# Attention scores with full-depth products per component

## The chip, the cores and the metric

The kernel runs on one core of one Trainium2 chip. The metric is the device time of one execution in microseconds, the median of several runs. The core has five engines with queues of their own: TensorE (PE, matmuls; its weight loads are listed apart as PEld), VectorE (DVE), ScalarE (ACT), GpSimd (POOL) and SyncE (SP), which issues most DMA transfers. Each engine takes its instructions in a fixed order.

## The reference, cut to what matters

The reference is a decoder layer on 1024 rows of 1024 channels: three branches for token mixing (differential attention, retention, a gated linear recurrence) merged by gates, then cross-attention, then an MLP. The change touches the scores of the differential attention. It has eight heads; each has two components of 64 channels for queries and keys and one value of 128 channels. For each block of 128 queries:

```python
s = jnp.einsum('bqhcd,bkhcd->bhcqk', q_blk, k).astype(jnp.float32) * scale
s = jnp.where(causal, s, -jnp.inf)
p = jax.nn.softmax(s, axis=-1)
a = p[:, :, 0] - lam * p[:, :, 1]
return jnp.einsum('bhqk,bkhe->bqhe', a.astype(v.dtype), v)
```

All of it is in float32. The kernel feeds TensorE with float32 numbers in two rounded parts (a "Split": hi and lo, whose sum is the number) and adds several products: for a plain product hi x hi, hi x lo and lo x hi.

## The kernel before, in words

`run` goes through the stages in order: retention, then `attention`, then the recurrence and the gates (`h_products`), the branch products, cross-attention and the MLP. Here only `attention` matters, from about 304 to 766 us of the trace.

`attention` goes over eight heads (h) and, in each, over eight query blocks of 128 rows (i). `diff_scores(h, i)` makes the two score matrices of a block, one for each component, of n = 128 (i + 1) columns, in accumulators of two PSUM banks each (tag "sc", two in all), adds the causal mask to the last 128 columns (L462), finds the row maximum (L464), takes the exponential into an SBUF tile of 4 KB per partition (tag "p", L467; the row sums come along), scales (L469, L472) and joins both components (L473). The joined matrix stays in the first component's tile until it is transposed. `diff_trans(h, j)` (L487) transposes the matrices of blocks 2j and 2j + 1 once both are there, in the step of block 2j + 2, for the last pair in the step of the next head's first block. `diff_av` multiplies with the values, `diff_out` normalises the result, with a few small transfers through DRAM.

The queries and keys of a head come from `diff_qk`: a projection of 24 products on 512 columns for each half of the rows, into PSUM tiles "psk". The keys are kept in tiles of 128 partitions (tag "kd"): for the first component hi in the lower 64 partitions and lo in the upper ones, for the second one the other way round (L430, L431). The queries (tag "qd", two tiles) hold three planes of 512 columns: hi of the first component twice, in both halves of the partitions, hi of the second likewise, and one plane with lo of both, the first component's in the lower 64 partitions, the second's in the upper ones. ACT writes hi (L441), DVE subtracts to get lo (L442), and a DMA on SP's queue copies hi to the other half of the partitions (L443).

So a score block of up to 512 columns takes four products. Two have depth 128 (L457), one for each component: hi of the queries, twice, against hi over lo of the keys. Two have depth 64 (L460): lo of the queries against hi of the keys, the first component's in partitions 0 to 63, the second's in 64 to 127.

Between the score steps the projections of the next head (`diff_qk`, `diff_v`) are put in at given blocks (`FILL`). The order in which each engine gets its instructions is not that of the code alone: a planner takes them by priority (the code's order) as its own model finds them ready, and gives out the places of the tile pools at the same time. A tile's place can be taken again when its last reader is through. `wdma`, `wsplit` and the like keep some instructions in the code's order.

Of the kernel before, what the change touches and what calls it, by code (L numbers as in the profile page):

```python
# [17 lines left out]
P = 128  # L18
# [7 lines left out]
# columns of the per-channel vector table  # L26
# [13 lines left out]
class Split:  # L40
    """An f32 operand as an exact sum of two f32r parts."""
# [8 lines left out]
class Kernel:  # L50
# [17 lines left out]
    def split(self, dst, src, lo_engine=None):  # L68
        """src f32 in SBUF or PSUM -> dst Split"""
        ins = self.nc.scalar.copy(dst.hi, src)  # L70
        self.lo_ins = (lo_engine or self.nc.vector).tensor_tensor(dst.lo, src, f32(dst.hi), op=ALU.subtract)  # L71
        return ins

    def after(self, key, ins):
        """keep the instructions of one key, all of one engine, in program order"""
        prev = self.last.get(key)
        if prev is not None:
            self.tc.add_manual_dep(
                ins.ins, prev.ins.name, mybir.DependencyInfo(mybir.DependencyClass.NoSync, mybir.DependencyReason.DATA),
                reason="program order")  # L80
        self.last[key] = ins

    def weight(self, unit, kts, pool=None, tag="w", wbufs=2, dst=None, lo=None):
        """a [128, 1024] weight unit -> Split of [128, kts, 1024 // kts]"""
        st = self.stage.tile([P, D], F32, tag="st", name="st")
        self.after("wdma", self.nc.sync.dma_start(st, unit))
        w = dst
        if dst is None:
            w = (pool or self.wpool).tile([P, 2, D], F32R, tag=tag, name=tag, bufs=None if pool is None else wbufs)
        s = Split(w[:, 0, :], w[:, 1, :])  # L90
        self.after("wsplit", self.split(s, st, lo or self.nc.gpsimd))
        return Split(*[p.rearrange("p (k c) -> p k c", k=kts) for p in (s.hi, s.lo)])

    def rstd(self, dst, src, scale, eps):
        """dst = (src * scale + eps) ** -0.5 on [128, few]"""
        self.nc.vector.tensor_scalar(dst, src, scale, eps, op0=ALU.mult, op1=ALU.add)
        self.nc.gpsimd.tensor_tensor(dst, dst, self.mhalf[:, : dst.shape[-1]], op=ALU.pow)

    def norm_rows(self, xt, gain, work, bufs=2):
        """normalise the rows of xt [128, 1024]"""  # L100
        nc = self.nc
        xs = work.tile([P, D], F32, tag="xs", name="xs", bufs=bufs)
        ss = self.small.tile([P, 1], F32, tag="ss", name="ss", bufs=4)
        nc.scalar.activation(xs, xt, AF.Square, accum_out=ss)
        rs = self.small.tile([P, 1], F32, tag="rs", name="rs", bufs=4)
        self.rstd(rs, ss, 1.0 / D, 1e-6)
        self.norm_ins = nc.vector.scalar_tensor_tensor(xs, xt, rs, gain, op0=ALU.mult, op1=ALU.mult)
        return xs

    def rows_T(self, xs, dst, psum, key=None):  # L110
        """xs [128, 1024] transposed into dst, two Splits [128, 4, 128]"""
# [9 lines left out]
    def later(self, f=None, depth=1):  # L121
        """put off f until the tensor engine has had other work; run what was put off before the last `depth`"""
        if f is not None:
            self.put_off.append(f)
        while len(self.put_off) > (depth if f is not None else max(0, len(self.put_off) - 1)):
            self.put_off.pop(0)()
            if f is None:
                break
# [39 lines left out]
    def scalars(self):  # L168
        """lambda of the differential attention, its output gains"""
# [20 lines left out]
    def softplus(self):  # L190
        """softplus of the LRU's parameter, times its factors"""
# [7 lines left out]
        # log1p(z) = 2 atanh(z / (2 + z)), 0 <= z <= 1  # L199
# [18 lines left out]
    def norm_x(self, work):  # L218
        """h^T, the normalised input; a generator, one step per 128 rows"""
# [21 lines left out]
    # retention, one chunk of one head at a time, in stages  # L241
    def ret_proj(self, h, n, c):
# [5 lines left out]
        # rotary  # L248
# [7 lines left out]
        # the keys' decay is put into the values, the queries' into the norm  # L256
# [43 lines left out]
    def ret_out(self, h, n, c):  # L300
# [3 lines left out]
        # group norm  # L304
# [28 lines left out]
    def retention(self, pool):  # L333
        """retention without its gate, led by the norm of its input"""
# [33 lines left out]
    def h_sums(self, kt, half, hp):  # L368
        """the sums of blocks of h^T that its block products need, to DRAM"""
# [26 lines left out]
    def proj_T(self, w, half, ps):  # L396
        """out^T [128 columns, 512 rows]"""
        self.mmk(ps, [(w[:, kt, :], self.hT[half][kt // 4][:, kt % 4, :]) for kt in range(KT)])

    # differential attention  # L400
    def diff_v(self, pr):
        """the projections of two heads' values, in four steps"""
# [13 lines left out]
    def diff_qk(self, h):  # L416
        """the projections of a head's queries and keys, in four steps"""
# [5 lines left out]
        for half in range(2):  # L423
            ps = self.ps.tile([P, HB], F32, tag="mm", name="psk")
            self.proj_T(w, half, ps)
            # of the first component hi over lo, of the second lo over hi
# [7 lines left out]
        for half in range(2):  # L434
            ps = self.ps.tile([P, HB], F32, tag="mm", name="psk")
            self.proj_T(w, half, ps)
            # hi of each component twice, lo of both
            t = ap.tile([P, 3, HB], F32R, tag="qd", name="qd", bufs=2)
            q.append(t)
            for c, (x, y) in enumerate(((lower, upper), (upper, lower))):  # L440
                nc.scalar.activation(t[x, c, :], ps[x, :], AF.Copy, scale=0.125)  # L441
                v.scalar_tensor_tensor(t[x, 2, :], ps[x, :], 0.125, f32(t[x, c, :]), op0=ALU.mult, op1=ALU.subtract)  # L442
                nc.sync.dma_start(f32(t[y, c, :]), f32(t[x, c, :]))  # L443
            yield

    def diff_scores(self, h, i):
# [7 lines left out]
        for b in range((n + HB - 1) // HB):  # L454
            e = min(HB, n - b * HB)
            for c, sc in enumerate(scs):
                nc.tensor.matmul(sc[:, b * HB:b * HB + e], lhsT=qt[:, c, cols], rhs=k[b][:, c, 0:e], start=True, stop=False)  # L457
            for c, sc in enumerate(scs):
                x = slice(64 * c, 64 * c + 64)
                nc.tensor.matmul(sc[:, b * HB:b * HB + e], lhsT=qt[x, 2, cols], rhs=k[b][x, c, 0:e], start=False, stop=True)  # L460
        for sc in scs:
# [3 lines left out]
            p = ap.tile([P, S], F32, tag="p", name="p", bufs=5)  # L465
# [80 lines left out]
    def attention(self):  # L546
# [18 lines left out]
        for h in range(8):  # L565
            # the rest of this head's projections, then the next one's
# [81 lines left out]
    def h_products(self):  # L648
        """the LRU's projections and scan, retention's gate, the merge gates: block products with h^T;
        a generator: the first two steps need no pools of their own"""  # L650
# [8 lines left out]
        # which sums of blocks of the branches' inputs go with which pair  # L659
# [80 lines left out]
    def o_sums(self, i, q, sp):  # L740
        """the sums of blocks of a branch's input that its block products need, to DRAM: T1, T3 and T4, T2"""
# [14 lines left out]
    def load_blocks(self, i, tile):  # L756
        """the right factors of a branch: even tiles of channels first, then odd ones; a generator, one step a block"""
# [13 lines left out]
    def fill_block(self, b, x, tile):  # L771
        """a [128, 4, 512] of DRAM, split"""
# [5 lines left out]
    def gates(self, count, pool, tag):  # L778
        """the next merge gates, to DRAM; two steps a gate"""
# [13 lines left out]
    def branch(self, order, i, right, bw, st, sps, nxt):  # L793
        """a branch's product, gated, added to those before it; then the next one's right factors, or the sum split"""
# [46 lines left out]
    def w_out(self, half, mT, w, hx, work, psum):  # L841
        """from here on to the last norm the second half of the rows comes first"""
# [22 lines left out]
    def block(self, pool):  # L865
        """a Split of [128, 4, 512]"""
# [3 lines left out]
    def mem_slot(self):  # L870
        kv, hm = (s.tile([P, 2, 2, D], F32R, tag="s", name="kvox") for s in (self.slotA, self.slotB))
        # keys, values; the normalised memory first, then the attention's output
# [29 lines left out]
    # cross-attention, one head of half the rows at a time, in stages  # L902
# [42 lines left out]
    def xa_out(self, st, cb, g):  # L945
        """half a tile of rows of the cross-attention's output, the MLP's norm"""
# [14 lines left out]
    # the MLP's right factors come from the even (B11, B21) and the odd (B12, B22) tiles of rows  # L961
# [26 lines left out]
    def mlp_t4(self, i, g):  # L988
        """T4 of a tile of rows, once there is room for it"""
# [8 lines left out]
    def xattn(self, hx, work, psum):  # L998
        """the memory's keys and values, the cross-attention; ends with rows still to transpose"""
# [7 lines left out]
        def SC(u):  # L1007
            """the scores of head u, the transposes of the one before"""
# [48 lines left out]
    # 2 x 2 block products with seven multiplications (Winograd's form);  # L1057
    # left factors: A11 A12 S4 A22 S1 S2 S3, right factors: B11 B21 B22 T4 T1 T2 T3, T4 with its sign turned
# [6 lines left out]
    def left(self, raw, s1, s2, s4, eng):  # L1065
        """the sums of the left factor's blocks; S3 takes the place of A21"""
# [16 lines left out]
    def pair(self, p, k, c, units, right, psum, emit, lo):  # L1083
        """product k of a pair of units, with its raw units and sums in place"""
# [19 lines left out]
    def product(self, k, c, right, psum, lo, emit):  # L1104
        """product k of a pair of 128-column tiles; emit(i, j, x, y) gets a block of the result as x + y"""
# [13 lines left out]
        # t0: P1, U2, U4; t1: U3  # L1119
# [18 lines left out]
    def mlp1(self, p, k, c):  # L1138
        """product k of the pair p of 128 hidden channels"""
# [9 lines left out]
        def emit(i, j, x, y):  # L1149
            """squared ReLU"""  # L1150
# [42 lines left out]
    def mlp2(self, c, acc, mps, gf):  # L1193
        """the second product over four tiles of hidden channels, added to the seven sums"""
# [40 lines left out]
    def out_rows(self, st, k, x, gf):  # L1235
        """the last norm; the first half of a row is there before the second"""
# [21 lines left out]
    def mlp_in(self):  # L1258
        """the squared ReLU of the first product, and the right factors of the second, to DRAM"""
# [65 lines left out]
def host_arrays(x, mem, norm_mix, w_in, diff_lq1, diff_lk1, diff_lq2, diff_lk2, diff_subln, lru_conv_w, lru_conv_b,  # L1325
# [4 lines left out]
    def units(w, kts):  # L1330
        """[K, C] -> [K / 128 / kts, 128, kts * C]"""
# [3 lines left out]
    def cols(w, width, kts):  # L1335
        """[K, C] -> [C / width, units, 128, kts * width]"""
# [4 lines left out]
    def halves(w):  # L1341
        """the even tiles of 128 rows before the odd ones"""
# [56 lines left out]
```

## Time and profile before

| | us |
|---|---|
| median of 3 runs (lowest, highest) | 2488.87 (2486.42, 2490.97) |
| profiled execution, its span | 2489.1 |
| PE busy | 2355.3 (95% of the span) |
| PE weight loads busy | 1906.0 (77%) |
| DVE busy | 1851.9 (74%) |
| ACT busy | 1042.4 (42%) |
| POOL busy | 1088.3 (44%) |

The span runs from the first to the last instruction of one profiled execution; the page gives no other time for that execution, and the span agrees with the median of the runs. Times in rows count from the span's start. A row of the timeline has the start, the time, the engine, the line of the kernel, the operation, what it writes and reads, rows and columns of the stationary operand (128*128 or 64*128), and the shape of the moving operand; "x2" stands for two instructions in a row that were merged, and in brackets is the idle time of the engine ahead of it with what ended it. Matmuls are pipelined: one starts long before the one ahead of it has ended, so their durations overlap.

### The profile page before, as it was taken

To read this page: it belongs to the slowest core of one execution; us is meant where nothing else is said; L and a number is where in the kernel's file an instruction comes from. 1 tells how busy PE (TensorE), PEld (TensorE's weight loads), DVE (VectorE), ACT (ScalarE), POOL (GpSimd) and SP (SyncE) were. 2 spreads that over 40 slices of the span, in tenths; PEclk is the share of its full clock that TensorE was granted. 3 is DMA by queue.
4 is the path that set the end of the run, shared out by engine and by line. 5 is a ranking of instruction groups with operands and counts; after the bars stand their busy time and mean duration, and the time that the engine had idled before them with its cause. 6 is when DMAs were issued, how large, how long until landed. Compare 5 with 4: busy or idle time off the path is not lost. (4 is left out here: it accounts for less than half of the span.)

```text
span 2489.1 us, 31236 instructions
## 1 busy us (share of the span) xinstructions
PE 2355.3 (95%) x11132; PEld 1906.0 (77%) x11132; DVE 1851.9 (74%) x2850; ACT 1042.4 (42%) x1823; POOL 1088.3 (44%) x714
## 2 busy tenths in 40 slices
PE   9999999999999999999998978899989999999996
PEld 7888878787876877777776767688768888778884
DVE  7577476767786777777677887534788888878888
ACT  5443344545455554454354443235442222343333
POOL 1122212221214555565553333225145555698787
PEclk9999999999999999999999989999999999999999
DMA  5222212122114435534576776434225444744432
GB/s 173 74 85 69 62 45 60 44 60 54 51 41 140 152 120 185 182 119 144 194 233 220 241 264 205 141 129 136 94 85 178 148 140 140 275 152 169 147 142 75
DMA packets 137259, 334.08 MB, mean 134 GB/s; under 512 B 17152, under 2 KB 27393, under 8 KB 137104
## 3 DMA queue, kind: packets, MB, share of 16 engines
q1 hardware_dynamic: 136528, 330.25, 40.2%
q8 instruction: 89, 1.46, 0.3%
q10 hardware_dynamic: 576, 1.84, 0.2%
q14 instruction: 66, 0.54, 0.1%
HBM read 229.21 MB, written 98.63 MB: 132 GB/s over the span
## 5 line engine op out<-in xcount | busy, mean ns | idle before, releaser
L59 PE MATMUL ps<-block,wu 128*128 128x512 f32 x1428 | 570.5, 400 | 55.6 <-DVE sf L1126 23.5
L61 PE MATMUL ps<-block,wu 128*128 128x512 f32 x1428 | 568.2, 398 | 16.7 <-POOL wu L71 10.2
L60 PE MATMUL ps<-block,wu 128*128 128x512 f32 x1428 | 565.0, 396 | 0.1
L71 POOL TENSOR_TENSOR wu<-st,wu 128x512 fp32r<-128x512 f32 x214 | 324.9, 1533 | 323.4 <-ACT wu L70 323.3
L59 PEld LDWEIGHTS ps<-block,wu 128*128 128x128 f32 x1428 | 273.2, 191 | 120.0 <-issue 19.6
L61 PEld LDWEIGHTS ps<-block,wu 128*128 128x128 f32 x1428 | 272.9, 191 | 85.5 <-POOL wu L71 15.8
L60 PEld LDWEIGHTS ps<-block,wu 128*128 128x128 f32 x1428 | 272.7, 191 | 60.7 <-DVE block L71 1.1
L70 ACT CAST wu<-st 128x512 fp32r<-128x512 f32 x240 | 141.5, 618 | 163.3 <-DVE st L1067 68.9
L59 PE MATMUL ps<-wu,hu 128*128 128x512 f32 x448 | 176.6, 394 | 15.6 <-DVE acc L1199 13.6
L71 POOL TENSOR_TENSOR w<-st,w 128x1024 fp32r<-128x1024 f32 x50 | 122.1, 2453 | 154.9 <-ACT w L70 137.5
L61 PE MATMUL ps<-wu,hu 128*128 128x512 f32 x448 | 174.9, 392 | 5.1 <-DVE hu L71 5.1
L60 PE MATMUL ps<-wu,hu 128*128 128x512 f32 x448 | 175.2, 391 | 0.1
L1199 DVE TENSOR_TENSOR acc<-acc,ps 128x512 f32<-128x512 f32 x216 | 137.8, 677 | 21.3 <-PE ps L61 20.6
L71 POOL TENSOR_TENSOR wu<-sf,wu 128x512 fp32r<-128x512 f32 x63 | 115.9, 1853 | 64.9 <-ACT wu L70 51.8
L71 DVE TENSOR_TENSOR hu<-sth,hu 128x1024 fp32r<-128x1024 f32 x56 | 122.1, 2185 | 20.6 <-ACT hu L70 20.2
L467 ACT ACTIVATE p<-sc,mx 128x256 f32<-128x256 f32 (+7 forms) x128 | 94.5, 740 | 65.8 <-DVE mx L464 61.9
L59 PEld LDWEIGHTS ps<-wu,hu 128*128 128x128 f32 x448 | 84.6, 189 | 38.9 <-DVE acc L1199 10.7
L59 PE MATMUL psk<-block,w 128*128 128x512 f32 x256 | 104.8, 409 | 0.0
L61 PEld LDWEIGHTS ps<-wu,hu 128*128 128x128 f32 x448 | 84.6, 189 | 23.5 <-DVE hu L71 6.0
L61 PE MATMUL psk<-block,w 128*128 128x512 f32 x256 | 101.8, 398 | 0.0
L60 PE MATMUL psk<-block,w 128*128 128x512 f32 x256 | 101.6, 397 | 0.0
L60 PEld LDWEIGHTS ps<-wu,hu 128*128 128x128 f32 x448 | 84.6, 189 | 17.8 <-POOL wu L71 0.5
(391 smaller groups left out, 5627.2 us busy)
## 6 DMA issues: line engine op xcount, KB each, us to landing
sth<-h SPq DMA_DIRECT2D x56, 512.0 KB, 8.9
st<-in_w SPq DMA_DIRECT2D x32, 512.0 KB, 4.3
h<-hab SPq DMA_DIRECT2D x32, 512.0 KB, 2.8
w<-in_w SPq DMA_DIRECT2D x8, 2048.0 KB
sgb<-gsp SPq DMA_DIRECT2D x48, 256.0 KB, 4.3
gsp<-l SPq DMA_DIRECT2D x44, 256.0 KB, 3.1
acc<-y SPq DMA_DIRECT2D x40, 256.0 KB, 4.2
st<-in_w_br SPq DMA_DIRECT2D x18, 512.0 KB, 6.4
```

Of the source, the lines that this page charges most:

```text
L59: nc.tensor.matmul(ps, lhsT=lhs.hi, rhs=rhs.hi, start=start, stop=False)
L60: nc.tensor.matmul(ps, lhsT=lhs.hi, rhs=rhs.lo, start=False, stop=False)
L61: nc.tensor.matmul(ps, lhsT=lhs.lo, rhs=rhs.hi, start=False, stop=stop)
L70: ins = self.nc.scalar.copy(dst.hi, src)
L71: self.lo_ins = (lo_engine or self.nc.vector).tensor_tensor(dst.lo, src, f32(dst.hi), op=ALU.subtract)
L467: nc.scalar.activation(p[:, 0:n], sc[:, 0:n], AF.Exp, bias=mx, accum_out=l)
L1199: eng.tensor_tensor(acc[k][:, st, :], acc[k][:, st, :], x if isinstance(x, bass.AP) else acc[x][:, st, :], op=ALU.add)
```

## The change

Queries get two planes for each component, hi and lo, both copied to the other half of the partitions. Each component's score block is the sum of two products of depth 128: hi of the queries (twice) against hi over lo of the keys, and lo of the queries (twice) against the same keys. The product lo x lo, left out before, is thereby included. Both products of a component now follow each other. The copy (one transfer per component and half) holds both planes, 256 KB in place of 128 KB, and reads what DVE wrote too. The query tiles grow from 6 to 8 KB per partition (two of them), and the tiles for the exponentials become four in place of five. Comments and docstrings are taken out as well, which changes nothing else.

```diff
-            t = ap.tile([P, 3, HB], F32R, tag="qd", name="qd", bufs=2)
+            t = ap.tile([P, 2, 2, HB], F32R, tag="qd", name="qd", bufs=2)
             q.append(t)
             for c, (x, y) in enumerate(((lower, upper), (upper, lower))):
-                nc.scalar.activation(t[x, c, :], ps[x, :], AF.Copy, scale=0.125)
-                v.scalar_tensor_tensor(t[x, 2, :], ps[x, :], 0.125, f32(t[x, c, :]), op0=ALU.mult, op1=ALU.subtract)
-                nc.sync.dma_start(f32(t[y, c, :]), f32(t[x, c, :]))
+                nc.scalar.activation(t[x, c, 0, :], ps[x, :], AF.Copy, scale=0.125)
+                v.scalar_tensor_tensor(t[x, c, 1, :], ps[x, :], 0.125, f32(t[x, c, 0, :]), op0=ALU.mult, op1=ALU.subtract)
+                nc.sync.dma_start(f32(t[y, c]), f32(t[x, c]))
...
             for c, sc in enumerate(scs):
-                nc.tensor.matmul(sc[:, b * HB:b * HB + e], lhsT=qt[:, c, cols], rhs=k[b][:, c, 0:e], start=True, stop=False)
-            for c, sc in enumerate(scs):
-                x = slice(64 * c, 64 * c + 64)
-                nc.tensor.matmul(sc[:, b * HB:b * HB + e], lhsT=qt[x, 2, cols], rhs=k[b][x, c, 0:e], start=False, stop=True)
+                for part in range(2):
+                    nc.tensor.matmul(sc[:, b * HB:b * HB + e], lhsT=qt[:, c, part, cols], rhs=k[b][:, c, 0:e],
+                                     start=part == 0, stop=part == 1)
...
-            p = ap.tile([P, S], F32, tag="p", name="p", bufs=5)
+            p = ap.tile([P, S], F32, tag="p", name="p", bufs=4)
```

## Rows read from the trace of the kernel before

**Rows 1.** Busy time by engine in the attention; us, PE, PEld, DVE, ACT, POOL, PEclk, DMA

```profile
304.00:766.00 462.00, 459.21 (x2502) 357.14 (x2500) 346.64 (x703) 226.99 (x482) 91.25 (x68) 1.00 0.19 50
```

**Rows 2.** Score products by line; duration in ns (least, median, most), starts, shapes

```profile
L457 PE MATMUL sc<-kd,qd x192: 218/394/504, 304.4 to 756.0; 128*128 128x512 f32 x96, 128*128 128x128 f32 x32, 128*128 128x256 f32 x32, 128*128 128x384 f32 x32
...
L460 PE MATMUL sc<-kd,qd x192: 322/466/502, 304.6 to 756.5; 64*128 64x512 f32 x96, 64*128 64x128 f32 x32, 64*128 64x256 f32 x32, 64*128 64x384 f32 x32
```

**Rows 3.** Timeline of PE around the first score products; start, time, operation

```profile
304.39 0.24 PE L457 MATMUL sc<-kd,qd 128*128 128x128 f32 x1
304.56 0.32 PE L460 MATMUL sc<-kd,qd 64*128 64x128 f32 x1
304.81 0.50 PE L59 MATMUL psk<-block,w 128*128 128x512 f32 x1
305.15 0.39 PE L60 MATMUL psk<-block,w 128*128 128x512 f32 x1
305.38 0.40 PE L61 MATMUL psk<-block,w 128*128 128x512 f32 x1
```

**Rows 4.** Timeline of PE, products of depth 128 and 64 in turn

```profile
705.52 0.48 PE L457 MATMUL sc<-kd,qd 128*128 128x512 f32 x1
705.93 0.50 PE L460 MATMUL sc<-kd,qd 64*128 64x512 f32 x1
706.36 0.50 PE L457 MATMUL sc<-kd,qd 128*128 128x512 f32 x1
706.79 0.50 PE L460 MATMUL sc<-kd,qd 64*128 64x512 f32 x1
707.22 0.39 PE L60 MATMUL oT<-aTs,vd 128*128 128x256 f32 x1
```

**Rows 5.** Timeline of PE, two products of depth 64 side by side

```profile
327.26 0.50 PE L460 MATMUL sc<-kd,qd 64*128 64x512 f32 x2
327.69 0.50 PE L457 MATMUL sc<-kd,qd 128*128 128x256 f32 x2
```

**Rows 6.** Timeline of PE, the last product of depth 64

```profile
756.47 0.49 PE L460 MATMUL sc<-kd,qd 64*128 64x512 f32 x1
756.89 0.39 PE L59 MATMUL oT<-aTs,vd 128*128 128x256 f32 x1
```

**Rows 7.** Windows as in group 1: heads 0, 1, 2 and 7

```profile
305.60:350.00 44.40, 44.40 (x196) 31.26 (x195) 35.43 (x77) 23.57 (x51) 6.02 (x4) 1.00 0.18 42
350.00:420.00 70.00, 69.06 (x437) 57.84 (x436) 50.36 (x99) 33.02 (x72) 16.01 (x11) 1.00 0.17 44
420.00:471.00 51.00, 51.00 (x247) 37.66 (x246) 38.93 (x81) 27.22 (x59) 9.48 (x8) 1.00 0.24 66
...
713.00:766.00 53.00, 53.00 (x259) 38.41 (x257) 42.45 (x83) 22.63 (x52) 8.41 (x9) 1.00 0.16 45
```

**Rows 8.** Waits of DVE, 304 to 766 us; us in total, times, longest

```profile
DVE r L469 <- ACT p L467: 34.1, 56, 1.0
DVE sc L462 <- PE sc L460: 22.3, 36, 1.6
```

**Rows 9.** Waits of ACT, 304 to 766 us

```profile
ACT aTs L70 <- PE tpa L487: 66.9, 46, 3.7
```

**Rows 10.** Timeline at head 1's block 1, exponential and transposes

```profile
359.85 0.47 ACT L467 ACTIVATE p<-sc,mx 128x256 f32<-128x256 f32 x1 [2.90 <-DVE mx L464]
...
363.77 0.55 PE L487 MATMUL tpa<-cm,p 128*128 128x128 f32 x3
```

**Rows 11.** DMA issues by line; size of each, median us to landing

```profile
qd<-qd SPq DMA_DIRECT2D x32, 128.0 KB, 2.2
```

**Rows 12.** Subtraction for the queries' lo, by line

```profile
L442 DVE SCALAR_TENSOR_TENSOR qd<-psk,qd x32: 669/688/695, 301.8 to 722.2; 64x512 fp32r<-64x512 f32 x32
```

**Rows 13.** Timeline from the queries' copy to head 1's first score product

```profile
342.54 0.47 SPq L443 DMA_DIRECT2D qd<-qd  x1
...
346.16 0.22 PE L457 MATMUL sc<-kd,qd 128*128 128x128 f32 x1
```

## The prediction

> **What bounds the kernel now.** Three views, in this order. The windows come first, one stretch for the attention and one on either side [rows 1]: the reader is to see that TensorE (PE) is busy for 459.2 of the 462 us, at the full granted clock (1.00, the 2.4 GHz level), and VectorE (DVE) for 346.6, ScalarE (ACT) for 227.0. So this stage ends when PE is through its queue, and whatever shortens that queue is worth its own length until DVE, at 75%, stands in the way. Busy says nothing of how well PE runs, so second comes the timeline of PE, read by the distance from one matmul's start to the next one's start; durations overlap and are of no use for a sum. A product of depth 128 on 512 columns steps by 0.23 us (305.15 to 305.38 [rows 3]), a 256-column one by 0.12, a 384-column one by 0.17, one of 128 columns by about 0.11. Third come the waits of DVE and ACT, to see who would hold PE back once it is faster.
>
> **What the score products cost now.** There are 192 products of full depth (L457) and 192 of depth 64 (L460), 96, 32, 32 and 32 of each at 512, 384, 256 and 128 columns [rows 2]. At the plain steps all 384 would take 192 x 0.229 + 64 x (0.172 + 0.119 + 0.108) = 69.5 us. Added up start to start over the whole trace they take 108.5 us. The 39.0 us between have a plain pattern. With full and half products in turn [rows 4] each of the four 512-column steps is 0.41 to 0.43 where 0.23 is plain: 1.70 us for 0.92. On 128 columns [rows 3] full to half takes 0.17, half to the next 0.25, and the next one, a 512-column projection, 0.34 where it has 0.23 elsewhere. The last half product of the stage shows the same [rows 6]: 0.42 to its successor. What the short depth gives back is seen in [rows 5]: where both components' halves stand side by side the trace merges them into one row (x2) of 0.50 us, as long as one alone in [rows 4]: they start 3 to 4 ns apart, and two cost one step. Counted over the trace (first [rows 3], last [rows 6]), the 192 halves come in 143 runs, 49 with two halves. Each run costs on average 0.12 us going in, 0.19 coming out and 0.09 on the matmul behind; of the last, 96 matmuls outside the scores hold 9.3 us that the 108.5 do not include. The pairs give back 49 x 0.174 = 8.5 us. Net 39.0 + 9.3 = 48.3 us of PE's time lies in changing depth.
>
> **The change, part by part.**
>
> *Products.* As many matmuls and weight loads as before, 384 each, all of depth 128, order per component high part, then low part. By the plain steps they take 69.5 us and the neighbours keep theirs: 48.3 us less on PE. Two products in a row into the same accumulator cost nothing extra, for the projections' three products per weight tile (L59 to L61) do just that at 0.23 [rows 3].
>
> *How much of it reaches the end.* From above: all 48.3, if the other engines' waits shrink along. From below: DVE's own waits on PE's scores are 22.3 us [rows 8]; if every wait of DVE for ACT stayed as long as it is, DVE would let the stage shrink by these 22.3 alone. I lie nearer the upper end, because those waits for ACT mostly pass on a wait for PE (ACT waited 66.9 us for transposes alone [rows 9]). By heads [rows 7], the surplus being 7.7 us in the first, 6.4 in each of heads 2, 4, 6, 4.7 in 1, 3, 5 and 6.9 in the last: the even heads would go from 51.0 to 44.6 us with DVE busy for 38.9 (87%), the odd ones from 70.0 to 65.3 with 50.4 (77%); but the first from 44.4 to 36.7 with 35.4 (96%), the last from 53.0 to 46.1 with 42.5 (92%). Over 90% an engine that works in order can't be fed without gaps, so I count half in those two, 7.3 of 14.6, and the rest in full: 48.3 - 7.3 = 41.0 us.
>
> *Four tiles for the exponentials, not five.* At an odd block the two matrices of the pair before must be transposed before their places are free, and the fifth tile covers for that. In 12 of the 64 blocks (seven of block 1, five of block 7) an exponential now starts before four places could have served it, by 2.2 to 5.3 us, 38 us in all. The middle one is in [rows 10]: the second exponential of block 1 at 359.85, the previous head's last transposes done at 364.32. Nothing lost as the lower end, 38 us as the upper one. At blocks 1 the next exponentials come 7 us or more later in most heads, with projections for PE in between, so delay is slack; the last head has the fewest projections to fill with. I take half of its two places (5.3 and 2.2): 3.8 us, rounded to 4.
>
> *The copies of the queries.* 32 transfers of 256 KB, not 128 KB, that now wait for DVE's subtraction (0.69 us each [rows 12]) as well as for ACT's copy. Before, they land 2.2 us after issue [rows 11]; twice the bytes should need between 2.2 and 4.4. So they land 0.7 to 2.9 us later. The tightest places are the first blocks of heads 1, 3, 5 and 7, where the second copy is issued 3.6 us before the first score product [rows 13], so 1.4 us lie between its landing and that product. Lower end 0; upper end 4 x 1.5 = 6 us, and as much as 9 if head 0's start loses too. I take 0: the first product reads the first component's copy, issued some 2 us earlier, and projections are there for PE meanwhile. What SP's queue holds behind is small transfers of the previous head's norm and a weight load, none of which PE waits for today.
>
> **Sum.** 41 - 4 = 37 us. The profiled execution has a span of 2489.1 us, the median of the runs is 2488.9, so 2452 us stands for both. The rest of the kernel (before 304 and after 766 us) keeps its instructions; the planner may order them anew, for which I allow 5 us either way.
>
> **A rule that speaks against it.** The Trainium skill, "TensorEngine Tiling (Array Packing)", section Overview (Theoretical Speedup), gives products of depth up to 64 up to twice the speed, since two halves of the array work at once. By it, if all 192 halves ran two by two and nothing else changed, the full-depth form would add half of their plain 34.7 us, and the sum would be 2489 + 17 = 2506 us. The trace bears it out for 49 pairs and no more. The same page, section Tiling Modes (Key Properties), says that a change of the mode drains the engine, which [rows 4] agree with.
>
> **Rivals.**
> (1) DVE takes over: only the 22.3 us come through, and up to 10 of them go to the four tiles: 2467 to 2477, middle 2470. For it: 92 to 96% in two heads; [rows 8] has 34.1 us of waiting on exponentials, which a faster PE doesn't shorten. Against it: 12 us of idle DVE in an even head, 20 in an odd one.
> (2) The whole 48 us and a little more, if the planner's order, made for steps without the surplus, now fits: 2436 to 2441.
> (3) The other side: the long steps come from something that stays, the way low and high products of one accumulator follow each other, and not from the depth. Then nothing is saved and the 49 pairs lose their common step: 2489 + 8.5 = 2497.5, and up to 2506 if all halves overlap somewhere that starts do not show. It decides if steps between full-depth score products stay near 0.41. Against it: [rows 3], where three products of one accumulator step plainly.
> (4) The four tiles stall PE itself: with only the 22.3 us gained and all 38 us of delays passed on through the two score accumulators, 2489 - 22 + 38 = 2505. It decides when PE waits at L457 for the exponential's result in most odd blocks. Against it: PE hardly waits there today, and projections are there to fill with in seven heads.
>
> **How the numbers follow.** The forecast 0.70 (its own range 2443 to 2463); rival (1) 0.15; (2) 0.08; (3) 0.04; (4) 0.03. The predicted time is 2452 us. The range 2439 to 2474 takes in most of (1) and (2); some 0.13 stay outside. This kernel tells 0.2%, about 5 us, from no change. Faster 0.92, same 0.02 (the upper edge of (1) with delays of (4)), slower 0.06 ((3), and nearly all of (4)).
>
> **What would show it.** Right: all score products of depth 128 with steps of 0.23, 0.17, 0.12 and 0.11; projections behind them at 0.23; PE's busy time in the stage some 40 us less, DVE's the same 347; even heads near 45 us, odd ones near 65. DVE's waits for L460's successor shrink. Wrong: PE idle before the scores, released by ACT's exponential (four tiles), by the copies' landing, or by DVE; or a time above 2475.

## The result, and the profile after

The changed kernel takes 2458.0 us (median of 4 runs, 2457.4 to 2459.0), before 2487.6 (4 runs, 2484.7 to 2491.0): ratio 0.9884, 95% interval 0.9870 to 0.9898, that is 28.9 us less (25.4 to 32.3). The forecast was 37 less, 2452, in a range from 2439 to 2474. The profiled span is 2455.6 us, for an execution of 2457.4; by the same 1.8 us the profiled execution of before, with its span of 2489.1, was one of the longer ones, near 2491. So the spans, 33.5 apart, overstate the gain a little.

The stage is best cut from the first score product to the matmul behind the last one. The row of before for 304.39 to 756.89 us and that of after for 305.70 to 725.85 have, in order, the length, the busy time of PE, PEld, DVE, ACT and POOL, the granted clock and DMA. First after:

```profile
305.70:725.85 420.15, 411.82 (x2442) 350.52 (x2441) 334.89 (x692) 225.05 (x476) 92.84 (x65) 1.00 0.24 63
```

Before, the same stage by the same view:

```profile
304.39:756.89 452.50, 449.71 (x2450) 349.44 (x2449) 339.54 (x693) 223.79 (x477) 89.41 (x67) 1.00 0.19 50
```

The stage lost 32.4 us, the rest of the kernel 1 (2036.6 to 2035.5). PE was busy for all but 2.8 us of it before and is idle for 8.3 now; the clock was full in both. The score products, by line (L458 in place of L457 and L460 [rows 2]) and in the timeline of PE at head 6, block 7, which answers to [rows 4]:

```profile
L458 PE MATMUL sc<-kd,qd x384: 220/387/504, 305.7 to 725.6; 128*128 128x512 f32 x96, 128*128 128x128 f32 x32, 128*128 128x256 f32 x32, 128*128 128x384 f32 x32
```

```profile
676.79 1.18 PE L458 MATMUL sc<-kd,qd 128*128 128x512 f32 x4
677.81 0.34 PE L59 MATMUL oT<-aTs,vd 128*128 128x256 f32 x1
677.98 0.40 PE L59 MATMUL psk<-block,w 128*128 128x512 f32 x1
```

Four products of 512 columns are through in 1.02 us (676.79 to 677.81), where they took 1.70. In both, some 0.08 us belongs to the start: the first product begins only 0.03 us behind the last of the transposes ahead of it, where 0.10 is plain. Over the stage the 384 products add up, start to start, to 77.5 us (108.5 before, 69.5 at plain steps), and the matmuls behind them have lost their surplus. But now PE waits for others. The waits of the weight loads (in all in us, times, longest in us):

```profile
PEld tpa L486 <- DVE aTs L71: 8.5, 21, 1.9
PEld sc L458 <- ACT p L466: 7.9, 18, 1.7
PEld ms L517 <- ACT s L70: 5.8, 14, 0.8
PEld tpa L486 <- DVE p L472: 4.1, 6, 1.4
PEld oT L59 <- ACT aTs L70: 3.4, 17, 0.3
```

Before, the two largest in its window were "issue" ahead of the score products, 38.7 us together, and none of them for another engine came above 2.3:

```profile
PEld sc L460 <- issue: 28.2, 101, 0.4
PEld sc L457 <- issue: 10.5, 43, 0.2
...
PEld tpa L487 <- DVE aTs L71: 1.2, 3, 0.4
```

The reader is to see one kind of row replaced by another: idle time that nothing outside PE explains is gone, and idle time released by DVE and ACT has come. DVE's wait for scores fell (22.3 us [rows 8], now 6.9). Its waits for ACT fell less: those for the transposed matrices, the values and the queries from 44.1 to 30.8 together, those for exponentials not at all. Before and after:

```profile
DVE r L469 <- ACT p L467: 33.6, 55, 1.0
...
DVE aTs L71 <- ACT aTs L70: 15.1, 29, 1.0
DVE vd L71 <- ACT vd L70: 14.8, 18, 1.6
DVE qd L442 <- ACT qd L441: 14.2, 16, 1.9
```

```profile
DVE r L468 <- ACT p L466: 33.8, 52, 1.2
DVE aTs L71 <- ACT aTs L70: 12.2, 16, 1.6
DVE vd L71 <- ACT vd L70: 10.4, 15, 1.4
DVE qd L442 <- ACT qd L441: 8.2, 16, 0.7
DVE sc L461 <- PE sc L458: 6.9, 11, 2.5
```

To compare kernels, the stage is taken apart by steps: each matmul's distance to the next one, less the plain step of its shape (0.229 us for 512 columns, 0.172, 0.119 and 0.108 for 384, 256 and 128, 0.104 for a transpose). What is over goes to "depth" (into a run of halves, out of it, and the matmul behind), to "pairs" (the step saved by two halves side by side), or to "rest", which is PE waiting. The rest after, 25.4 us, is more than the 8.3 us of idle time above, since a matmul's row is longer than its plain step (0.39 us for 0.23) and covers short waits. "Plain" differs by some us where a few matmuls moved over the edges of the stage. All twelve experiments are in the table; the parts are in us, and the time is the ratio's, with its interval, against before on the same chip. As a gauge of the stage's noise, e10 has the changed kernel's order on PE and its stage to within 0.1 us, e11 that of e9 to within 0.7.

| kernel | runs of halves | stage | plain | depth | pairs | rest | time against before |
|---|---|---|---|---|---|---|---|
| before | 143 | 452.5 | 396.4 | 56.5 | -8.5 | 8.1 | |
| after | 0 | 420.1 | 394.8 | 0 | 0 | 25.4 | -28.9 (-32.3 to -25.4) |
| e1 depth alone | 0 | 421.1 | 396.4 | 0 | 0 | 24.7 | -33.5 (-37.7 to -29.1) |
| e2 e1, four tiles | 0 | 419.1 | 396.4 | 0 | 0 | 22.7 | -31.3 (-36.0 to -26.8) |
| e3 before, four tiles | 143 | 450.5 | 396.4 | 56.6 | -8.5 | 6.0 | +1.0 (-1.5 to +3.5) |
| e4 e1, other order | 0 | 424.0 | 396.4 | 0 | 0 | 27.6 | -25.1 (-28.8 to -21.4) |
| e5 no pairs | 191 | 478.2 | 396.4 | 75.7 | -0.2 | 6.4 | +25.4 (+21.9 to +28.8) |
| e6 halves grouped | 101 | 437.9 | 396.4 | 36.0 | -4.1 | 9.7 | -14.2 (-17.4 to -10.9) |
| e7 grouped and kept | 75 | 431.8 | 398.3 | 27.6 | -12.5 | 18.4 | -21.9 (-25.4 to -18.4) |
| e8 after, scaling on ACT | 0 | 421.2 | 394.5 | 0 | 0 | 26.6 | -31.1 (-34.8 to -27.4) |
| e9 after, shorter split | 0 | 429.2 | 395.0 | 0 | 0 | 34.2 | -20.4 (-24.1 to -16.6) |
| e10 after, maximum not used | 0 | 420.1 | 394.8 | 0 | 0 | 25.3 | -26.6 (-31.3 to -21.9) |
| e11 e9 and e10 | 0 | 429.9 | 395.0 | 0 | 0 | 34.9 | -19.1 (-22.6 to -15.4) |
| e12 two places | 0 | 445.6 | 395.0 | 0 | 0 | 50.6 | -5.0 (-7.7 to -2.0) |

### The profile page after: what moved, and what is told of

Its sections match the earlier page's. It is cut to its first block, busy times and chain, and to the rows that moved or that the text cites. A ratio compares the mean times of both kernels' runs of the same rounds, so it can differ in the third digit from the quotient of the medians.

```text
span 2455.6 us, 31231 instructions
## 1 busy us (share of the span) xinstructions
PE 2320.9 (95%) x11132; PEld 1908.8 (78%) x11132; DVE 1854.2 (76%) x2850; ACT 1044.8 (43%) x1823; POOL 1091.8 (44%) x714
## 5 line engine op out<-in xcount | busy, mean ns | idle before, releaser
L1198 DVE TENSOR_TENSOR acc<-acc,ps 128x512 f32<-128x512 f32 x216 | 137.8, 678 | 20.4 <-PE ps L61 19.9
L466 ACT ACTIVATE p<-sc,mx 128x256 f32<-128x256 f32 (+7 forms) x128 | 94.8, 741 | 71.1 <-DVE mx L463 49.2
L61 PEld LDWEIGHTS ps<-wu,hu 128*128 128x128 f32 x448 | 84.7, 189 | 22.6 <-DVE hu L71 4.9
L60 PEld LDWEIGHTS ps<-wu,hu 128*128 128x128 f32 x448 | 84.7, 189 | 17.2 <-POOL wu L71 0.4
```

Source lines behind the costliest of these rows:

```text
L60: nc.tensor.matmul(ps, lhsT=lhs.hi, rhs=rhs.lo, start=False, stop=False)
L61: nc.tensor.matmul(ps, lhsT=lhs.lo, rhs=rhs.hi, start=False, stop=stop)
L466: nc.scalar.activation(p[:, 0:n], sc[:, 0:n], AF.Exp, bias=mx, accum_out=l)
L1198: eng.tensor_tensor(acc[k][:, st, :], acc[k][:, st, :], x if isinstance(x, bass.AP) else acc[x][:, st, :], op=ALU.add)
```

## The experiments

### Is it the depth alone? (e1)

```diff
-                x = slice(64 * c, 64 * c + 64)
-                nc.tensor.matmul(sc[:, b * HB:b * HB + e], lhsT=qt[x, 2, cols], rhs=k[b][x, c, 0:e], start=False, stop=True)
+                nc.tensor.matmul(sc[:, b * HB:b * HB + e], lhsT=qt[:, 2, cols], rhs=k[b][:, c, 0:e], start=False, stop=True)
```

> The kernel before with only the depth changed: the second product takes all 128 partitions of the plane with both lo parts, against hi over lo of the keys (it adds the other component's lo x lo, which the reference has not). Copies of 128 KB, five tiles for the exponentials, order of the products as before. My theory (changing depth costs PE 48 us; of that the changed kernel loses some 8 to the four tiles and the rest to DVE's chain): 2443 to 2452 us, score steps of 0.23 us. Rival 'DVE takes what is missing, the four tiles nothing': 2456 to 2460, as the changed kernel. Rival 'the gain comes from the copies or the order, not the depth': 2480 or more.

It took 33.5 us off, with tiles and copies as before. The order is as before too: in both traces PE, DVE, ACT and POOL have the same instructions in the same order, 11132 of them matmuls, and only the depth differs. So the depth is the cause of the whole gain; the rival of copies or order falls. But its stage (421.1) is no shorter than the changed kernel's (420.1), so what is missing of the 48 us was not taken by the changed kernel's other edits, nor by a new order. At 2452.8 us the run lies just above my range, and my expectation of some 8 us for the four tiles began to fall here.

### The four tiles (e2, e3)

e2 has this edit on top of e1's, e3 alone:

```diff
-            p = ap.tile([P, S], F32, tag="p", name="p", bufs=5)
+            p = ap.tile([P, S], F32, tag="p", name="p", bufs=4)
```

> As e1, with four tiles for the exponentials. My theory: 2454 to 2460, 6 to 10 us more than e1, ACT's exponentials waiting for transposes and for DVE's joining of the components (about 18 us in all, as in the changed kernel). Rival 'DVE alone': within 2 us of e1.

> The kernel before with four tiles for the exponentials and nothing else changed. My theory (PE's own surplus covers delays of ACT there): 2487 to 2492, 0 to 4 us above before. Rival 'the fifth tile is worth the same anywhere': 2494 to 2498.

Both stages are 2.0 us shorter with four tiles, the times within each other's intervals. So the fifth tile was worth nothing here: e3 came out as I expected, and I was wrong on e2. ACT does wait for tiles, as forecast and at the place that was named: in the changed kernel's rows of ACT

```profile
ACT p L466 <- DVE p L472: 11.7, 5, 2.7
...
ACT p L466 <- PE tpa L486: 5.7, 5, 1.3
```

that makes 17 us of an engine busy for 225 of 420, and its wait cost nothing here. The planner, which gives out the tiles, gave PE another order in places (111 of the 2448 matmuls of the stage, in e2 as in e3); that this made room for the wait is my reading, not shown.

### The order of the products (e4)

The edit is shown against e1:

```diff
             for c, sc in enumerate(scs):
-                nc.tensor.matmul(..., lhsT=qt[:, c, cols], ...)
-            for c, sc in enumerate(scs):
-                nc.tensor.matmul(..., lhsT=qt[:, 2, cols], ...)
+                for plane in (c, 2):
+                    nc.tensor.matmul(..., lhsT=qt[:, plane, cols], ...)
```

> As e1, with the products in the changed kernel's order: both products of a component, then both of the other. My theory: within 3 us of e1, as steps don't depend on the order. Rival 'the order matters, by DVE getting the first component 0.2 to 0.5 us earlier in each of 64 blocks': 5 us or more below e1.

The stage is 2.9 us longer than e1's, the time 8.4 us, with 0.3 us between the two intervals; I had expected no more than 3. The rival (5 us or more faster) falls. The changed kernel's order costs some microseconds in place of saving any; how many, and why, is not settled.

### More and fewer changes of depth (e5, e6, e7)

If the surplus is the price of changing depth, the time must follow the number of changes while depth 64 stays. e5 gives each component's full and half product in turn; e6 all full products of a block, then all halves; e7 is e6 with the score products kept in the code's order on PE.

```diff
# e5
             for c, sc in enumerate(scs):
+                x = slice(64 * c, 64 * c + 64)
                 nc.tensor.matmul(..., lhsT=qt[:, c, cols], rhs=k[b][:, c, 0:e], start=True, stop=False)
-            for c, sc in enumerate(scs):
-                x = slice(64 * c, 64 * c + 64)
                 nc.tensor.matmul(..., lhsT=qt[x, 2, cols], rhs=k[b][x, c, 0:e], start=False, stop=True)
# e6
-        for b in range((n + HB - 1) // HB):
-            e = min(HB, n - b * HB)
+        bs = [(b, min(HB, n - b * HB)) for b in range((n + HB - 1) // HB)]
+        for b, e in bs:
             for c, sc in enumerate(scs):
                 nc.tensor.matmul(..., lhsT=qt[:, c, cols], ...)
+        for b, e in bs:
             for c, sc in enumerate(scs):
# e7: e6, and
-                nc.tensor.matmul(...)
+                self.after("sc", nc.tensor.matmul(...))
```

> The kernel before with its products of depth 128 and 64, given in the order full, half for one component and then for the other: on PE the 192 halves come in 191 runs (143 before), one pair in place of 49. Theory A (each run of halves costs PE 0.39 us, each pair gives back 0.174): 48 x 0.39 + 48 x 0.174 = 27 us above before, up to that much if PE sets the end. Theory B (what is saved comes from elsewhere, changes of depth are nearly free): 8 us, the pairs alone.

> The kernel before, still with depth 64, but all full products of a block first and then all its halves: 101 runs of halves, of which 54 hold two, three or four. Theory A: 42 x 0.39 = 16.5 us less for fewer changes and 3.5 for more pairs, 20 us below before (10 if DVE's chain takes half). Theory B: within 4 us of before.

> As e6, and the score products are kept in the code's order on PE: 75 runs of halves, 66 with two to four. Theory A: 68 x 0.39 + 39 x 0.174 = 33 us less on PE, so 20 to 31 below before, near the full-depth form's 31, the depth staying 64. Theory B: within 4 us of before or above it, for a score product that is held back holds back PE.

Measured: 25.4 above before (27 expected), 14.2 and 21.9 below (20, or 10 if DVE's chain takes half, and 20 to 31 expected). In PE's steps each run of halves costs 0.396 us in e5 (75.7 / 191), 0.395 in before (56.5 / 143), 0.356 in e6 and 0.368 in e7: one price over a range of 75 to 191. Theory B falls. In e5's timeline of PE,

```profile
334.86 0.50 PE L459 MATMUL sc<-kd,qd 64*128 64x512 f32 x1
335.29 0.44 PE L458 MATMUL sc<-kd,qd 128*128 128x384 f32 x1
335.66 0.43 PE L459 MATMUL sc<-kd,qd 64*128 64x384 f32 x1
336.02 0.50 PE L59 MATMUL psk<-block,w 128*128 128x512 f32 x1
336.36 0.39 PE L517 MATMUL ms<-s,onesr 128*128 128x512 f32 x1
```

each step is 0.34 to 0.43 us. In e7's

```profile
457.12 0.73 PE L461 MATMUL sc<-kd,qd 64*128 64x512 f32 x4
457.78 0.39 PE L59 MATMUL oT<-aTs,vd 128*128 128x256 f32 x1
```

four halves of 512 columns together take 0.66 us, the change back to full depth included, where one alone with its change back takes 0.43 (334.86 to 335.29). With the way in and the matmul behind counted too, such a run (there are five in e7) is 0.05 us cheaper than four full products at plain steps. Every other kind of run in before, e5, e6 and e7 is dearer on average: by 0.16 to 0.35 us for two halves of 512 columns, by 0.40 to 0.53 for one.

The table's column "rest" shows where the gain went: 6.4, 8.1, 9.7, 18.4 and 24.7 us for 191, 143, 101, 75 and no runs of halves (e5, before, e6, e7, e1). While PE was slowed down by its changes of depth, the others' results were there in time; each microsecond taken off that surplus is worth nearly a full one at first and about half of one at the end. From e5 to before the stage lost 25.7 us of 27.5 taken off depth and pairs, from before to e6 14.6 of 16.1, from e6 to e1 16.8 of 31.9. e7 lies between those two and not on a straight line (6.1 of the first 16.8, then 10.7 of 15.1); it alone also holds the score products in the code's order.

### DVE's load (e8)

```diff
-        nc.vector.tensor_scalar(pc[1][:, 0:n], pc[1][:, 0:n], rc[1], self.nlam, op0=ALU.mult, op1=ALU.mult)
+        nc.vector.tensor_scalar(rc[1], rc[1], self.nlam, None, op0=ALU.mult)
+        nc.scalar.activation(pc[1][:, 0:n], pc[1][:, 0:n], AF.Copy, scale=rc[1])
```

> The changed kernel with the scaling of the second component's matrix (64 instructions, 42 us of DVE in the stage) moved to ACT, and 64 products of one column left on DVE (some 10 us). Theory C (DVE's load is what keeps 16 of the 48 us): 5 to 12 us below the changed kernel, PE's waits for DVE's splits and joins (17 us) down by half. Theory D (it is the chain from one engine to the next, not the load): within 3 us, or above, as ACT's exponentials stand behind the scaling.

The window of its stage:

```profile
305.34:726.50 421.16, 413.03 (x2441) 350.63 (x2440) 310.97 (x693) 269.14 (x539) 93.47 (x67) 1.00 0.24 63
```

DVE has 24 us less to do than in the changed kernel, ACT 44 more, and the stage is 1.0 us longer. The time (31.1 below before) can't be told from the changed kernel's 28.9. So theory C's forecast, 5 to 12 us less, fails, and theory D's holds. PE's waits for DVE's splits and joins, on matmuls and weight loads, went from 17.2 to 13.1 us, not down by half, and its waits for ACT from 21.0 to 24.0. A lighter DVE gained nothing here; but the run doesn't part that from a busier ACT, and PE's order changed with it.

### The chains (e9 to e12)

Theory D1 was that single steps of the chain from engine to engine hold PE: the one PSUM place of the transposes, which is free only when DVE has read it, or the exponentials behind the row maximum.

```diff
# e9
-            self.split(t[:, 0:len(blocks), :], tp[:, 0:len(blocks), :])
+            s, nb = t[:, 0:len(blocks), :], tp[:, 0:len(blocks), :]
+            self.nc.scalar.copy(s.hi, nb)
+            self.nc.vector.tensor_tensor(s.lo, f32(s.hi), f32(s.hi), op=ALU.subtract)
# e10
-            nc.scalar.activation(p[:, 0:n], sc[:, 0:n], AF.Exp, bias=mx, accum_out=l)
+            nc.scalar.activation(p[:, 0:n], sc[:, 0:n], AF.Exp, bias=self.eps5, scale=0.01, accum_out=l)
# e11: both
# e12
-            if (h, j) != (7, 3):
+            if (h, j) != (7, 3) and g % 2 == 1:
+                tp = self.ps.tile([P, 4, P], F32, tag="mm", name="tpm")
+            elif (h, j) != (7, 3):
```

> The changed kernel, where DVE's part of the transposed matrices is taken from ACT's part in SBUF (it comes out as zero, so lo of these matrices is left out), with as many DVE instructions as before, but the one PSUM place of the transposes is free once ACT has read it. Theory D1 (PE waits for that one place: 11 us in the changed kernel's rows): 5 to 11 us below the changed kernel, 2447 to 2453. Rival D2 (another wait takes its place): within 3 us of it.

> The changed kernel with an exponential that doesn't wait for the row maximum (a constant and a scale of 0.01 in its place; the maximum is still taken, by as many DVE instructions, and not used). Theory D1 (the single accumulator per component and the four tiles wait on exponentials, 9.6 us of PE's waits at the scores): 5 to 10 us below the changed kernel. Rival D2: within 3 us.

> e9 and e10 together: DVE's load as in the changed kernel, both chains shortened. If chains and not loads hold what is missing of the 48 us, the stage's 420 us go to 403 to 408 and the time to 2441 to 2446. If it stays above 2452, what is missing lies neither in DVE's load (e8) nor in these chains.

> The changed kernel, complete, with every second group of transposes put into a PSUM place of the projections (two of those), so that the next group needn't wait for the split of the one before. Theory D1: PE's 11 us of waits for splits shrink, 3 to 8 us below the changed kernel. Rival D2: the projections wait for their places in turn, within 3 us or above.

None was faster than the changed kernel. e9 leaves out the low part of the transposed matrices, e10 and e11 the row maximum; e12 leaves out nothing. In e9 the transposes' wait for DVE's split is gone, as it had to be, and others are larger; the waits of its weight loads:

```profile
PEld sc L458 <- ACT p L466: 16.1, 31, 1.7
PEld tpa L486 <- ACT aTs L490: 11.7, 40, 0.8
```

With a shorter chain the planner gave another order (1580 of the changed kernel's 2441 matmuls keep their sequence on PE), and the stage is 9 us longer. So the run shows that the edit gains nothing, not that the wait it removed was harmless. e10 did not cut what it was to cut: by its rows

```profile
ACT p L466 <- DVE mx L463: 48.8, 56, 2.8
```

ACT waits for DVE's maximum as long as in the changed kernel (49.2), though it no longer uses it; both read the same accumulator, and I take it that they are kept in order for that. Its stage, 420.1 us, is the changed kernel's. So e10 and the second half of e11 say nothing on the maximum. e12 traded the transposes' wait for the split (11.0 us, now 2.0) for a worse one, of transposes for a projection's place that DVE had yet to read:

```profile
PE tpm L488 <- DVE qd L442: 6.9, 4, 1.8
PE sc L458 <- ACT p L466: 4.9, 11, 1.3
```

and its stage is 25 us longer, again in another order. The form that the experiments point to is e1 or e2, the three planes with the full depth: as fast as the changed kernel by intervals that overlap, with half its bytes copied. Its price is a term that the reference has not, lo x lo of the other component.

## Why the prediction was right or wrong

*The surplus of changing depth, 48.3 us:* right. All score products have one depth, their steps are plain where PE doesn't wait, the matmuls behind them too. With nothing but the depth changed, e1 has none of the 48.0 us that the table gives for depth and pairs before, and e5 to e7 give the same price of 0.36 to 0.40 us a run while depth 64 stays (0.12 + 0.19 + 0.09 in the prediction).

*How much reaches the end, 41.0 us:* this is the term that was mis-sized. The stage lost 32.4 us. PE's waiting grew from 8.1 to 25.4 us, 17 in place of the 7.3 that I allowed. I allowed it in the two heads where DVE would be over 90% busy and counted all other heads in full; it came as 5.9 us in those two and 11.3 in the six others. How much each head gave is best read from e1, since in the changed kernel work moved over the heads' boundaries (its last head has 211 matmuls for 228). Heads 1 and 2 from first score product to first score product, before and in e1:

```profile
346.16:418.21 72.05, 71.11 (x446) 59.37 (x444) 52.11 (x102) 33.92 (x71) 14.22 (x10) 1.00 0.18 45
418.21:467.01 48.80, 48.80 (x239) 36.01 (x238) 37.17 (x80) 26.17 (x55) 11.27 (x9) 1.00 0.24 66
```

```profile
340.79:410.34 69.55, 67.59 (x446) 60.24 (x445) 52.55 (x103) 34.20 (x71) 14.76 (x10) 1.00 0.17 47
410.34:454.44 44.10, 43.85 (x238) 36.17 (x238) 35.43 (x79) 26.03 (x55) 12.09 (x9) 1.00 0.28 73
```

Head 1 gave 2.5 us of its 4.7 and head 2 4.7 of 6.3, and the other odd and even heads gave the same. The first and the last head gave 9.8 of 14.7, two thirds, and the six that I counted in full 21.6 of 33.2, two thirds as well. The smallest share came in the odd heads, where DVE is least busy (76%, for 80% in the even ones and 87 and 88% in the first and the last). So DVE's occupancy was the wrong gauge, and no run shows a limit at 90%. The reason that I gave for lying near the upper end holds in small part only: DVE's waits for ACT in the stage fell from 83.0 to 71.1 us, and those for exponentials stayed. The bounds, 22.3 and 48.3, held.

*Four tiles, 4 us:* wrong, nothing, by e2 and e3; the waits are on ACT, and PE doesn't see them.

*The copies:* right. They land later than before, and nothing on PE waits for them:

```profile
qd<-qd SPq DMA_DIRECT2D x32, 256.0 KB, 2.9
```

2.9 us (2.2 before [rows 11], 2.2 to 4.4 expected), and neither the rows of PE nor those of PEld name them.

*The sum:* 37 us forecast; 28.9 by the ratio, 33.5 by the spans, 32.4 by the stage. The error is 10 us too little waiting, partly made good, by luck, by 4 us too much for the tiles. Rival (1), that DVE's chain keeps more than half, had the right direction for the missing part and too much of it; PE now waits for ACT (21.0 us, weight loads and matmuls) at least as much as for DVE (17.2). Rival (2), the whole 48 us and more, falls by the time. Rival (3) falls by e1, and by e5 to e7 the 2506 us that the prediction worked out from doubled speed. The speed of up to twice that the Trainium skill ("TensorEngine Tiling (Array Packing)", section Overview) gives for such products shows in the pairs, which start 3 to 4 ns apart; but here each run of halves must pay 0.4 us for the change, more than the 0.17 that a pair gives back. Rival (4) falls by e2 and e3. One of the signs that I named for being wrong does show in part: PE waits at the scores for ACT's exponential, 9.6 us (7.9 on weight loads, 1.7 on matmuls), and 4.0 in e1 with five tiles.

*What stays open:* which of the waits makes up the 17 us. A new order is not needed for it, for in e1 the order stayed and the waits grew by 16.6 us. The tiles are excluded by e2. In e1 the largest growth is in the transposes' wait for DVE's split of the ones before, 1.2 us before:

```profile
PEld tpa L486 <- DVE aTs L71: 8.6, 22, 0.9
```

e9 and e12 took this wait away and e8 a part of DVE's load, and none gained; but each changed PE's order, by as much as the effect sought, so they don't clear what they touched. A run with one wait removed and the order kept was not tried.

## What to carry to other kernels

Read an engine's steps start to start, by shape: a busy share of 99% hid 48 us, a tenth of this stage. Half-depth products between full ones hardly pay even in groups, since the change costs some 0.4 us a run and a pair gives back one step: of all kinds of runs here, only four halves of 512 columns came out ahead, by 0.05 us. When a bound engine is relieved, its own surplus has been hiding waits for the others: here that took a third of the gain, so don't expect the whole of it, nor the occupancy of the next engine to tell where.

## What the runs showed of the hardware

The price of a change of depth spreads over three matmuls, and the one behind it, of full depth, carries 0.1 us of it (0.34 us for 0.23 [rows 3]). That one's row is longer too, 0.50 us for 0.39 or 0.40, but durations show only this part of the price. Two halves side by side cost one step, and four in a run two (0.66 us in e7 for 0.46 at plain steps, the change back included).
